# An S5 layer whose inputs and scan states are re-laid by DMAs through DRAM instead of transposes

## The chip, the cores and the metric

The kernel runs on one core of a Trainium2 chip. TensorE multiplies matrices, VectorE and ScalarE work on tiles elementwise, GpSimd does little arithmetic here and issues some of the DMAs, SyncE (SP) issues most of them. Each engine takes its own instructions in their written order and waits on semaphores. The metric is the device time of one execution in microseconds; before the change its median of three runs is 1847.47 us (1845.74 to 1847.80).

## The reference

Two layers over 256 frames of width 2048: gated linear attention, then an S5 state-space layer. The change touches the S5 layer alone:

```python
proj = u_in @ w_in                     # 2048 -> 8192
u, z = jnp.split(proj, 2, axis=-1)     # 4096 each
...
# per group of 16 channels (256 groups, 64 complex states each)
bu = einsum('blgi,gpi->blgp', u_b, B_bar)      # real and imaginary part
x  = associative_scan(x_t = lambda * x_(t-1) + bu_t)
y  = einsum(x_r, c_re) - einsum(x_i, c_im) + d_skip * u
y  = gelu(y)
y  = y * sigmoid(y @ w_glu + b_glu)
y  = y * silu(z)
return y @ w_out                        # then gate, residual, LayerNorm
```

All is float32. A large product is computed from a high part (a rounded copy) and a low part of each operand as three matmuls: high x high, high x low, low x high.

## The kernel before

**Streams of weights.** Each projection runs over groups of 512 output columns. A *step* (a k-pair) loads 512 KB of weights on SP's queue (wload), makes the high part by a ScalarE cast (L145) and the low part by a VectorE subtraction (L146), and then runs 24 TensorE matmuls of 128x256 into four PSUM banks (st_step, L180 to L182). Three buffers each hold high and low parts, so a cast can run three steps ahead of TensorE. S5 has a u stream (tiles wsu, hisu, su; eight groups of eight steps) and then a z stream (wsz, hisz, sz; the same), then the GLU (gl) and the output projection (op).

**The S5 core beside the streams.** The 256 frames are cut into 32 chunks of 8. Index f (0 to 31) stands for 8 channel groups, 128 rows in all. During the u stream:
- s_in copies each u bank out of PSUM with a VectorE transpose (L1108, tile vv), and s_in2, one or two steps later, re-lays it by four TensorE transposes (L1116, psu) and a ScalarE copy (L1118) into Ut, where the 8 frames of a chunk and 16 channels lie on the 128 partitions and the chunks on the free side.
- b_pow and b_tr make the powers of the state matrix times B; s_mm (L1129, L1134) multiplies them with U and writes the chunks' inputs into the state array sx; k_out sends the 8-frame convolution kernel to DRAM (dk) from GpSimd.
- a list of steps is worked off beside the weight steps: bstep takes b_pace of them, pump takes others (scan) at SCAN_RATE.

During the z stream from its second group on, pump works off a list at Y_RATE entries a step. For each f it holds three scan steps (while there are any), cside (loads the convolution matrix mt and the rows cl, and makes the output powers wc on VectorE), xstage and ystage. xstage(f) takes the states of f out of sx by a VectorE transpose (L1245, xT), two TensorE transposes (L1248, psxs) and a ScalarE copy (L1250, xS). ystage(f), two list rounds later, does 48 small matmuls (psy: mt with U at L1260, wc with xS at L1263), a VectorE transpose (yt) and a ScalarE gelu back into Ut. A *y group* is these 48 matmuls, a *state pair* the two transposes. Each z group of four banks ends in four ScalarE silu copies (zs, L1290).

A scheduler, not the source alone, sets the order on each engine: it places an instruction when its inputs are ready by its own estimate. The orders shown below are those of the built programs.

## Time and profile before

| what | value |
| --- | --- |
| median of runs | 1847.47 us |
| span of the profiled execution | 1844.7 us |
| TensorE busy | 1795.5 us (97%) |
| VectorE busy | 1422.5 us (77%) |
| ScalarE busy | 897.4 us (49%) |
| GpSimd busy | 72.7 us (4%) |
| u stream (767.6 to 1036 us) | 268 us |
| z stream (1036 to 1296 us) | 260 us |
| GLU (1296 to 1657 us) | 361 us |

The profiled execution is one run of the program; all durations come from it, and its span, from the first to the last instruction, is 2.8 us under the median of the timed runs. A TensorE instruction's busy time overlaps the next one's: a 128x256 matmul lasts 0.28 us while the following one starts 0.12 us after it. So TensorE time is counted here from start to start.

### The profile page before, as it was taken

To read this page: it belongs to the slowest core of one execution; us is meant where nothing else is said; L and a number is where in the kernel's file an instruction comes from. 1 tells how busy PE (TensorE), PEld (TensorE's weight loads), DVE (VectorE), ACT (ScalarE), POOL (GpSimd) and SP (SyncE) were. 2 spreads that over 40 slices of the span, in tenths; PEclk is the share of its full clock that TensorE was granted. 3 is DMA by queue.
4 is the path that set the end of the run, shared out by engine and by line. 5 is a ranking of instruction groups with operands and counts; after the bars stand their busy time and mean duration, and the time that the engine had idled before them with its cause. 6 is when DMAs were issued, how large, how long until landed. Compare 5 with 4: busy or idle time off the path is not lost.

```text
span 1844.7 us, 33886 instructions
## 1 busy us (share of the span) xinstructions
PE 1795.5 (97%) x13619; PEld 1588.5 (86%) x13619; DVE 1422.5 (77%) x1890; ACT 897.4 (49%) x1252; POOL 72.7 (4%) x78
## 2 busy tenths in 40 slices
PE   7999999999999999999999999999999999999997
PEld 5776897899999888899999999988888888888885
DVE  4877657879989888697899689888677775557556
ACT  5433557556556333654454454545544444444332
POOL 0000000000000000002223200000000000000000
PEclk9999999999999999999999999999999999999999
DMA  9996875889889998465654477899688886668653
GB/s 343 386 333 248 294 244 164 279 261 325 291 286 317 333 353 281 163 220 158 183 151 147 139 214 222 235 246 238 224 276 264 276 271 206 191 189 325 194 184 92
DMA packets 243798, 449.48 MB, mean 244 GB/s; under 512 B 19572, under 2 KB 48942, under 8 KB 242358
## 3 DMA queue, kind: packets, MB, share of 16 engines
q1 hardware_dynamic: 239320, 436.02, 73.9%
q0 software_dynamic: 3552, 10.24, 1.8%
q8 instruction: 107, 1.75, 0.4%
q10 hardware_dynamic: 768, 1.05, 0.2%
q14 instruction: 51, 0.42, 0.1%
HBM read 432.81 MB, written 14.42 MB: 242 GB/s over the span
## 4 chain that ended last, share of the span: by engine, by line
PE 86%; DVE 8%; DMA 3%; ACT 2%; issue 2%; SPq 0%; DVEq 0%; ACTq 0%
PE gl L192 13%; PE gl L193 7%; PE op L168 6%; PE op L167 6%; PE op L169 6%; PE z L182 3%; PE z L180 3%; PE z L181 3%; PE sz L180 3%; PE v L168 3%; PE v L169 3%; PE sz L181 3%; PE sz L182 3%; PE v L167 3%; PE su L180 2%; PE su L182 2%
## 5 line engine op out<-in xcount | busy, mean ns | idle before, releaser
L146 DVE TENSOR_TENSOR logl<-wgl,higl 128x1024 fp32r<-128x1024 f32 x128 | 156.5, 1224 | 115.3 <-ACT higl L145 113.7
L145 ACT CAST higl<-wgl 128x1024 fp32r<-128x1024 f32 x128 | 134.4, 1051 | 172.2 <-PE gl L192 167.9
L192 PE MATMUL gl<-yb,higl 128*128 128x512 f32 x512 | 179.6, 395 | 0.0
L192 PE MATMUL gl<-yp,higl 128*128 128x512 f32 x512 | 179.3, 395 | 0.1
L145 ACT CAST hio<-wo 128x1024 fp32r<-128x1024 f32 x95 | 100.2, 1055 | 155.3 <-PE op L169 127.3
L146 DVE TENSOR_TENSOR loo<-wo,hio 128x1024 fp32r<-128x1024 f32 x95 | 116.2, 1225 | 67.2 <-ACT hio L145 63.7
L315 DVE SCALAR_TENSOR_TENSOR acc<-wa,cs,acc 128x512 f32<-128x512 f32 x217 | 162.2, 748 | 4.8 <-DMA wa<-in_ada_w 2.1
L180 PE MATMUL su<-u1h,hisu 128*128 128x256 f32 x512 | 153.5, 301 | 1.9 <-DVE vv L1108 1.9
L180 PE MATMUL sz<-u1h,hisz 128*128 128x256 f32 x512 | 149.7, 292 | 1.2 <-ACT zs L1290 1.2
L180 PE MATMUL z<-u0h,hiz 128*128 128x256 f32 x512 | 148.7, 290 | 0.0
L182 PE MATMUL su<-u1h,losu 128*128 128x256 f32 x512 | 145.7, 286 | 0.4 <-DVE losu L146 0.4
L181 PE MATMUL su<-u1l,hisu 128*128 128x256 f32 x512 | 145.8, 285 | 0.0
L182 PE MATMUL z<-u0h,loz 128*128 128x256 f32 x512 | 144.9, 283 | 0.6 <-DVE loz L146 0.6
L182 PE MATMUL sz<-u1h,losz 128*128 128x256 f32 x512 | 144.9, 283 | 0.0
L181 PE MATMUL sz<-u1l,hisz 128*128 128x256 f32 x512 | 144.7, 283 | 0.0
L181 PE MATMUL z<-u0l,hiz 128*128 128x256 f32 x512 | 144.7, 283 | 0.0
L193 PE MATMUL gl<-yb,logl 128*128 128x256 f32 x512 | 143.4, 280 | 0.0
L193 PE MATMUL gl<-yp,logl 128*128 128x256 f32 x512 | 142.0, 280 | 0.0
L145 ACT CAST hisz<-wsz 128x1024 fp32r<-128x1024 f32 x64 | 66.9, 1051 | 107.2 <-PE sz L181 55.1
L192 PEld LDWEIGHTS gl<-yb,higl 128*128 128x128 f32 x512 | 96.0, 188 | 22.6
L192 PEld LDWEIGHTS gl<-yp,higl 128*128 128x128 f32 x512 | 95.8, 188 | 22.6 <-issue 0.6
L145 ACT CAST hisu<-wsu 128x1024 fp32r<-128x1024 f32 x64 | 66.7, 1050 | 95.1 <-PE su L181 70.6
(322 smaller groups left out, 5019.8 us busy)
## 6 DMA issues: line engine op xcount, KB each, us to landing
wgl<-in_s_w_glu SPq DMA_DIRECT2D x128, 512.0 KB, 4.7
wa<-in_ada_w SPq DMA_DIRECT2D x116, 512.0 KB, 5.1
wv<-in_gla_w_in SPq DMA_DIRECT2D x64, 512.0 KB, 6.1
wz<-in_gla_w_in SPq DMA_DIRECT2D x64, 512.0 KB, 5.2
wsu<-in_s_w_in SPq DMA_DIRECT2D x64, 512.0 KB, 3.7
wsz<-in_s_w_in SPq DMA_DIRECT2D x64, 512.0 KB, 4.3
wo<-in_s_w_out SPq DMA_DIRECT2D x64, 512.0 KB, 4.5
a<-in_ada_w SPq DMA_DIRECT2D x31, 1024.0 KB, 10.7
```

The lines of the kernel that those rows point to most:

```text
L145: S.copy(hi, w)
L146: last_lo[0] = V.tensor_tensor(lo, w, hi.bitcast(F32), op=ALU.subtract).ins
L167: PE.matmul(banks[tt], lhsT=uh, rhs=hi[:, kk, :], start=(k == first), stop=False)
L168: PE.matmul(banks[tt], lhsT=uh, rhs=lo[:, kk, :], start=False, stop=False)
L169: last_mm[0] = PE.matmul(banks[tt], lhsT=ul, rhs=hi[:, kk, :], start=False, stop=(k == last)).ins
L180: PE.matmul(o, lhsT=wh, rhs=u.hi(k), start=(k == first), stop=False)
L181: PE.matmul(o, lhsT=wh, rhs=u.lo(k), start=False, stop=False)
L182: last_mm[0] = PE.matmul(o, lhsT=wl, rhs=u.hi(k), start=False, stop=(k == last)).ins
L192: PE.matmul(banks[f], lhsT=hi[:, kk, fs], rhs=u.both(k), start=(k == 0), stop=False)
L193: PE.matmul(banks[f][:, :T], lhsT=lo[:, kk, fs], rhs=u.hi(k), start=False, stop=(k == last))
L315: V.scalar_tensor_tensor(acc[0], w[:, kk, :], cs[:, k:k + 1], acc[0], op0=ALU.mult, op1=ALU.add)
```

## The change

**u.** s_in now takes a whole group of four banks. Four ScalarE copies put them, frames within the chunk outermost, into vv (one buffer in place of two); GpSimd issues a DMA of vv to a DRAM scratch du (512 KB) and, when that has landed, a DMA from du into Ut in the wanted layout (runs of 512 bytes). s_in2, its transposes and its copy are gone. Ut's free side is laid out otherwise, so s_mm, ystage and the GLU's conversions address it anew. b_pace starts at -4.0 in place of -1.0, so that s_mm of a group comes three steps later.

**States.** xstage becomes xwrite and xread. xwrite(f) copies the states of f out of sx on ScalarE, with a stride, into xT (one buffer) and GpSimd writes them to the scratch dx (128 KB); xread(f) reads them back into xS (three buffers, runs of 256 bytes). xwrite stands one round ahead of xread, and xread two ahead of ystage. Y_RATE rises from 2.311 to 2.9, as the list grows from 126 entries to 158. yt has one buffer in place of two.

**Rows.** The new layout has another order of the output rows, so rec gets a copy of c's rows with its halves swapped (two more GpSimd writes for each of two halves of the groups), and cload takes one DMA in place of three.

```diff
-    rec = dp.tile([P, 32, 384], F32, name="rec")
+    rec = dp.tile([P, 32, 512], F32, name="rec")
 
     dk = dp.tile([512, 1920], F32, name="dk")
     dxn = dp.tile([T, D], F32, name="dxn")
+    dx = dp.tile([32, P, 256], F32, name="dx")
+    du = dp.tile([8, P, 1024], F32, name="du")
...
-        wdma(rec[:, 16 * t:16 * t + 16, 128:256], lc.rearrange("p f r g n -> p f (r g n)"))
+        wdma(rec[:, 16 * t:16 * t + 16, 256:384], lc.rearrange("p f r g n -> p f (r g n)"))
...
+                if o == 128:
+                    for h in range(2):
+                        wdma(rec[64 * h:64 * h + 64, 16 * t:16 * t + 16, 0:128], av[64 - 64 * h:128 - 64 * h])
...
-    Y_RATE = 2.311
+    Y_RATE = 2.9
...
-    Ut = [s8t(f"U{i}", [8, 2, 128]) for i in range(4)]
+    Ut = [s8t(f"U{i}", [2, 8, 4, 32]) for i in range(4)]
+
+    def Uv(f):
+        return Ut[f // 8][:, (f % 8) // 4, :, f % 4, :]
...
-    def s_in(p, banks):
-
-        v = tp.tile([P, 2, 2, 16, 8], F32, tag="vv", name=f"vv{p}", bufs=2)
-        for i in range(2):
-            V.transpose(v[:, i].rearrange("p b i s -> p s b i"),
-                        banks[i][:, :T].rearrange("p (s b i) -> p s b i", s=8, b=2)[:, ::-1])
-        return v
-
-    def s_in2(p, v):
-        pu = psx(f"psu{p}")
-        for i in range(2):
-            for b in range(2):
-                PE.transpose(pu[:, (2 * i + b) * P:(2 * i + b + 1) * P], v[:, i, b].rearrange("p i s -> p (i s)"), ident)
-        U = Ut[p // 4][:, 2 * (p % 4):2 * (p % 4) + 2]
-        S.copy(U.rearrange("p f b r -> p (f b r)"), pu)
+    def s_in(g, banks):
+
+        v = tp.tile([P, 8, 4, 32], F32, tag="vv", name=f"vv{g}", bufs=1)
+        for i in range(4):
+            S.copy(v[:, :, i], banks[i][:, :T].rearrange("p (s c) -> p s c", s=8)[:, ::-1])
+        wdma(du[g], v.rearrange("p s f c -> p (s f c)"))
+        wdma(Ut[g // 2][:, g % 2].rearrange("p g f c -> p g (f c)"),
+             du[g].rearrange("(g i) (s x) -> (i s) g x", i=16, s=8))
...
-            U = Ut[f // 8][:, f % 8]
+            U = Uv(f)
...
-                    PE.matmul(pss[i][32 * q:32 * q + 32, b * P:(b + 1) * P], lhsT=U[:, b, 32 * q:32 * q + 32],
+                    PE.matmul(pss[i][32 * q:32 * q + 32, b * P:(b + 1) * P], lhsT=U[:, 2 * q + b],
...
-                b_pace[0] = -1.0
+                b_pace[0] = -4.0
...
-        vs.extend((2 * g + i, s_in(2 * g + i, banks[2 * i:2 * i + 2])) for i in range(2))
+        s_in(g, banks)
...
-        dma(a[:, 0:256], rec[:, f, 0:256])
-        for h in range(2):
-            dma(a[64 * h:64 * h + 64, 256:384], rec[64 - 64 * h:128 - 64 * h, f, 0:128])
+        dma(a, rec[:, f, 0:384].rearrange("(r l) x -> l r x", r=4))
...
-    def xstage(f):
-        xt_ = tp.tile([P, 2, 4, 32], F32, tag="xt", name=f"xT{f}", bufs=1)
+    def xwrite(f):
+        xt_ = tp.tile([P, 4, 2, 32], F32, tag="xt", name=f"xT{f}", bufs=1)
         n = 2 * (f % 16)
-        V.transpose(xt_, sx[:, f // 16, 0:32, :, n:n + 2].rearrange("p c r b -> p b r c"))
-        px = psx(f"psxs{f}")
-        for b in range(2):
-            PE.transpose(px[:, b * P:(b + 1) * P], xt_[:, b].rearrange("p r l -> p (r l)"), ident)
-        xs = tp.tile([P, 2, 128], F32, tag="xs", name=f"xS{f}", bufs=2)
-        S.copy(xs, px[:, :T].rearrange("p (b r) -> p b r", b=2))
-        xss[f] = xs
+        S.copy(xt_, sx[:, f // 16, 0:32, :, n:n + 2].rearrange("p c r b -> p r b c"))
+        wdma(dx[f], xt_.rearrange("p r b c -> p (r b c)"))
+
+    def xread(f):
+        xs = xss[f] = tp.tile([P, 4, 2, 32], F32, tag="xs", name=f"xS{f}", bufs=3)
+        wdma(xs.rearrange("p q b c -> p q (b c)"), dx[f].rearrange("(q l) (r x) -> (l r) q x", q=4, r=4))
...
-                    PE.matmul(o[32 * q:32 * q + 32], lhsT=xs[:, b, 32 * q:32 * q + 32],
+                    PE.matmul(o[32 * q:32 * q + 32], lhsT=xs[:, q, b],
...
-        yt = tp.tile([P, 8, 32], F32, tag="yt", name=f"yt{f}", bufs=2)
+        yt = tp.tile([P, 8, 32], F32, tag="yt", name=f"yt{f}", bufs=1)
...
-                if 1 <= f < 33:
-                    bg.append(lambda f=f: xstage(f - 1))
+                for i in range(0 if f == 0 else f + 1, min(f + 2, 32)):
+                    bg.append(lambda i=i: xwrite(i))
+                if f < 32:
+                    bg.append(lambda f=f: xread(f))
...
-                hilo(pr[:, :, 0, :], pr[:, :, 1, :], ysrc[kp // 4][:, sl, :])
+                ph = pr.rearrange("p f h (t c) -> p f h t c", c=32)
+                yu = Ut[kp // 4][:, kp // 2 % 2, :, 2 * (kp % 2):2 * (kp % 2) + 2].rearrange("p t f c -> p f t c")
+                hilo(ph[:, :, 0], ph[:, :, 1], yu)
...
-                    V.tensor_tensor(zs[kp - 12], zs[kp - 12], ysrc[kp - 12], op=ALU.mult)
+                    for h in range(2):
+                        zv = zs[kp - 12][:, 4 * h:4 * h + 4].rearrange("p f (t c) -> p f t c", c=32)
+                        V.tensor_tensor(zv, zv, Ut[kp - 12][:, h].rearrange("p t f c -> p f t c"), op=ALU.mult)
```

The built program has 64 psu and 64 psxs transposes fewer on TensorE, 64 transposes fewer on VectorE and 64 DMAs fewer on SP, and 84 DMAs more on GpSimd.

First place: ScalarE at the end of the third u group (su2). Before, where kT and ks belong to k_out and s_mm and U is written elsewhere from psu:

```order
L145 CAST hisu27_8648<-wsu27_8646 128x1024
L1142 COPY kT2_8319<-pss4_8285 128x256
L1142 COPY kT2_8319<-pss5_8286 128x256
L1153 COPY ks1_8467<-psk1_8462 128x128 x2
L145 CAST hisu30_8701<-wsu30_8699 128x1024
L145 CAST hisu31_8776<-wsu31_8774 128x1024
L1102 COPY wbt4_8584<-pswb80_8585 128x512
```

Now, with the four copies of the finished banks into vv:

```order
L145 CAST hisu32_8733<-wsu32_8731 128x1024
L1143 COPY kT2_8399<-pss4_8365 128x256
L1143 COPY kT2_8399<-pss5_8366 128x256
L1154 COPY ks1_8541<-psk1_8536 128x128 x2
L1116 COPY vv2_8618<-su20_8186 128x8x32
L1116 COPY vv2_8618<-su21_8187 128x8x32
L1116 COPY vv2_8618<-su22_8188 128x8x32
L145 CAST hisu33_8776<-wsu33_8774 128x1024
L1116 COPY vv2_8618<-su23_8189 128x8x32
L1093 COPY wb4_8663<-rb4_8434 128x128 x2
L145 CAST hisu34_8845<-wsu34_8843 128x1024
```

The copies stand after casts of the next group (hisu30 to hisu32), and one cast, hisu33, stands ahead of the last copy. GpSimd's du write and the read into U1 wait for them.

Second place: ScalarE in the z stream, around the last steps of group 4. Before:

```order
L145 CAST hisz44_12974<-wsz44_12972 128x1024
L1267 ACT_TABLE_LOAD
L1267 ACTIVATE U0_7508<-yt7_12772 128x256
L1250 COPY xS9_12820<-psxs9_12817 128x256
L145 CAST hisz45_13042<-wsz45_13040 128x1024
L1267 ACTIVATE U1_7509<-yt8_12847 128x256
L1250 COPY xS10_12895<-psxs10_12892 128x256
L145 CAST hisz46_13117<-wsz46_13115 128x1024
L1267 ACTIVATE U1_7509<-yt9_12922 128x256
L1250 COPY xS11_12970<-psxs11_12967 128x256
L145 CAST hisz47_13182<-wsz47_13180 128x1024
L145 CAST hisz50_13238<-wsz50_13236 128x1024
```

Now, with copies out of sx (xT) that run ahead of the y groups (U<-yt8 and U<-yt9 belong to y groups 8 and 9):

```order
L145 CAST hisz43_12816<-wsz43_12814 128x1024
L1241 COPY xT17_13164<-sx_7511 128x256
L145 CAST hisz44_12884<-wsz44_12882 128x1024
L1262 ACTIVATE U1_7515<-yt8_12699 128x8x32
L1241 COPY xT18_13235<-sx_7511 128x256
L145 CAST hisz45_12947<-wsz45_12945 128x1024
L1241 COPY xT19_13336<-sx_7511 128x256
L1241 COPY xT20_13407<-sx_7511 128x256
L145 CAST hisz46_12988<-wsz46_12986 128x1024
L1262 ACTIVATE U1_7515<-yt9_12800 128x8x32
L1241 COPY xT21_13478<-sx_7511 128x256
L145 CAST hisz47_13056<-wsz47_13054 128x1024
```

The copies from psxs, one for each y group, are gone; the copies xT are closer together than the y groups are, since five of them, xT17 to xT21, stand between hisz43 and hisz47 beside the gelus of two y groups. Each of them waits for the DMA that empties xT. All of xT0 to xT15 stand between the 12th and the 28th cast of the z stream and all of xT16 to xT31 between the 35th and the 48th.

Third place: GpSimd's queue in the same stretch, where nothing stood before:

```order
L1242 DMA dx_200<-xT22_13579 128x256
L1246 DMA xS14_13016<-dx_200 128x4x64
L1242 DMA dx_200<-xT23_13658 128x256
L1242 DMA dx_200<-xT24_13759 128x256
L1246 DMA xS15_13087<-dx_200 128x4x64
L1242 DMA dx_200<-xT25_13830 128x256
L1246 DMA xS16_13167<-dx_200 128x4x64
L1242 DMA dx_200<-xT26_13901 128x256
L1242 DMA dx_200<-xT27_14002 128x256
L1242 DMA dx_200<-xT28_14073 128x256
L1246 DMA xS17_13268<-dx_200 128x4x64
L1242 DMA dx_200<-xT29_14153 128x256
```

Writes of dx and reads of xS alternate. A read waits for its write's landing and for the y group that frees its buffer, three y groups back, and the writes behind it wait with it.

More of the change, by code (lines that the diff above doesn't have):

```diff
@@ L1049, in bload @@
         a = tp.tile([P, 2, 384], F32, tag="rb", name=f"rb{f2}", bufs=2)
-        dma(a[:, :, 0:256], rec[:, 2 * f2:2 * f2 + 2, 128:384])
+        dma(a[:, :, 0:256], rec[:, 2 * f2:2 * f2 + 2, 256:512])
         for h in range(2):
-            dma(a[64 * h:64 * h + 64, :, 256:384], rec[64 - 64 * h:128 - 64 * h, 2 * f2:2 * f2 + 2, 256:384])
+            dma(a[64 * h:64 * h + 64, :, 256:384], rec[64 - 64 * h:128 - 64 * h, 2 * f2:2 * f2 + 2, 384:512])
         rb[f2] = a
@@ L1059, in kload @@
         a = rc[f2] = tp.tile([P, 2, 144], F32, tag="rc", name=f"rc{f2}", bufs=2)
-        dma(a, rec[:, 2 * f2:2 * f2 + 2, 0:144])
+        dma(a, rec[:, 2 * f2:2 * f2 + 2, 128:272])
     wb = {}
@@ L1190, in scan @@
         V.tensor_tensor(N, N, t1[:, 0], op=ALU.add)
-    vs = []
     for g in range(8):
@@ L1199, in trunk @@
             st_step(banks, u1, w, kp, 15)
-            if kp in (0, 2) and vs:
-                s_in2(*vs.pop(0))
             if (g, kp) == (0, 3):
@@ L1280, in trunk @@
             st_step(banks, u1, w, kp, 15)
-            if kp in (0, 2) and vs:
-                s_in2(*vs.pop(0))
             if g == 0:
@@ L1325, in trunk @@
                + [yb[:, i * 2048:(i + 1) * 2048].rearrange("p (k h t) -> p k h t", k=4, h=2) for i in range(4)])
-    ysrc = [u.rearrange("p f b r -> p f (b r)") for u in Ut]
     y2 = Parts([], [])
```

11 lines of the change are left out of this document (5 added, 6 removed).

## The prediction

> **What bounds the kernel now.** I read four views in this order: the chain of waits, the table of stretches, the waits inside the S5 projections, and single timeline stretches of TensorE and GpSimd. The chain comes first because it says whose work sets the end; then one row for each of three stretches of the S5 layer (u projection; first z group; the seven z groups beside which the y matmuls run). Their columns: stretch, its length, busy time of PE, PEld, DVE, ACT and POOL, granted clock, DMA share, GB/s.
>
> ```profile
> PE 86%; DVE 8%; DMA 3%; ACT 2%; issue 2%; SPq 0%; DVEq 0%; ACTq 0%
> ...
> 767.60:1036.00 268.40, 264.04 (x2805) 252.13 (x2803) 239.43 (x327) 137.87 (x250) 51.93 (x49) 0.99 0.56 171
> 1036.00:1069.00 33.00, 32.96 (x368) 31.48 (x366) 15.45 (x17) 17.07 (x33) 11.40 (x15) 1.00 0.44 131
> 1069.00:1296.00 227.00, 220.53 (x2937) 208.20 (x2937) 204.73 (x286) 117.06 (x176) 0.00 (x0) 1.00 0.88 231
> ```
>
> TensorE is idle for 4.4 us of 268 in the u stage and 6.5 of 227 in the y stage. A TensorE instruction taken out there shortens the program by its own pitch, as long as nothing else becomes late. VectorE is second (239 of 268, 205 of 227), ScalarE is half idle, GpSimd idle in the y stage.
>
> **What leaves TensorE.** Three timeline stretches: a u transpose group (L1116), a state transpose pair (L1248) alone, and a pair ahead of a y group.
>
> ```profile
> 842.33 0.28 PE L182 MATMUL su<-u1h,losu 128*128 128x256 f32 x1
> 842.45 0.60 PE L1116 MATMUL psu<-ident,vv 128*128 128x128 f32 x4
> 842.81 0.36 PE L180 MATMUL su<-u1h,hisu 128*128 128x256 f32 x1
> 843.01 0.28 PE L181 MATMUL su<-u1l,hisu 128*128 128x256 f32 x1
> ...
> 1186.56 0.28 PE L182 MATMUL sz<-u1h,losz 128*128 128x256 f32 x1
> 1186.68 0.38 PE L1248 MATMUL psxs<-ident,xT 128*128 128x128 f32 x2
> 1186.82 0.36 PE L180 MATMUL sz<-u1h,hisz 128*128 128x256 f32 x1
> 1187.02 0.28 PE L181 MATMUL sz<-u1l,hisz 128*128 128x256 f32 x1
> ...
> 1177.09 0.28 PE L182 MATMUL sz<-u1h,losz 128*128 128x256 f32 x1
> 1177.21 0.38 PE L1248 MATMUL psxs<-ident,xT 128*128 128x128 f32 x2
> ...
> 1178.97 0.38 PE L180 MATMUL sz<-u1h,hisz 128*128 128x256 f32 x1
> 1179.19 0.28 PE L181 MATMUL sz<-u1l,hisz 128*128 128x256 f32 x1
> ```
>
> Projection matmuls start 0.12 us apart (842.33 to 842.45). The u group delays them by 843.01 - 842.33 - 2 x 0.12 = 0.44 us, and there are 16: 7.0 us. A state pair costs 1187.02 - 1186.56 - 0.24 = 0.22 us, and there are 32: 7.0 us. **14.0 us** of TensorE time goes.
>
> For later: one step (a k-pair, 24 projection matmuls) takes 24 x 0.12 = 2.88 us, and a y group costs 1179.19 - 1177.09 - 0.24 = 1.86 us with its pair, so 1.64 without.
>
> With the transposes go some waits. These rows are from the waits of the S5 projections.
>
> ```profile
> PE pswb L1101 <- DVE wb L1092: 1.9, 2, 1.4
> PE su L180 <- DVE vv L1108: 1.9, 1, 1.9
> PEld psy L1260 <- ACT xS L1250: 1.9, 1, 1.9
> PE psxs L1248 <- DVE xT L1245: 1.2, 2, 0.8
> ```
>
> The last three name removed instructions: 1.9 + 1.9 + 1.2 = **5.0 us**. The first is VectorE's backlog; VectorE loses two groups (below), so some of its 1.9 may go too, but I count none.  Gross gain: **19.0 us**.
>
> **What moves to other engines.** Rows by line for the removed VectorE and ScalarE work, and what the z stream keeps on ScalarE:
>
> ```profile
> L1245 DVE STREAM_TRANSPOSE xT<-sx 128x256 f32<-128x256 f32 x32 | 20.1, 627 | 1.2 <-PE psxs L1248 0.9
> L1108 DVE STREAM_TRANSPOSE vv<-su 128x256 f32<-128x256 f32 x32 | 19.4, 665 | 0.7 <-PE su L182 0.7
> L1250 ACT COPY xS<-psxs 128x256 f32<-128x256 f32 x32 | 11.5, 361 | 2.0 <-PE psxs L1248 2.0
> L1118 ACT COPY U<-psu 128x512 f32<-128x512 f32 x16 | 9.3, 579 | 0.0
> L145 ACT CAST hisz<-wsz 128x1024 fp32r<-128x1024 f32 x53 | 55.4, 1051 | 92.1 <-PE sz L181 48.8 <-issue 36.2 <-DMA wsz<-in_s_w_in 3.5
> L146 DVE TENSOR_TENSOR losz<-wsz,hisz 128x1024 fp32r<-128x1024 f32 x53 | 64.0, 1210 | 7.9 <-ACT hisz L145 6.9 <-PE psy L1260 0.6
> L1267 ACT ACTIVATE U<-yt 128x256 f32<-128x256 f32 x32 | 13.3, 416 | 6.5 <-DVE yt L1266 6.4
> L1267 ACT ACT_TABLE_LOAD x10 | 12.8, 1283 | 5.3 <-DVE yt L1266 5.2
> L1290 ACT ACTIVATE zs<-sz 128x256 f32<-128x256 f32 x25 | 9.1, 387 | 3.9 <-PE sz L182 3.4
> ```
>
> VectorE loses 39.5 us that were beside TensorE; this is cover, not gain. ScalarE's sums hardly change: 32 PSUM copies of 128x256 at the 0.36 of L1250 (11.6 us) for the 9.3 of L1118, and 32 copies out of sx for the 11.5 of L1250. I cost four edits at nothing. The zs product in halves (four instruction starts more) and the y conversions in rows of 32 lie beside the GLU's and the last z group's matmuls; were they bare, four starts of a few tenths each. The four added writes of rec lie beside the v projection, and nothing reads rec before the S5 layer; bare, each is a 512 KB write of some 5 us (below), 20 in all. SP issues 64 loads fewer, beside weights it had loaded in time. What counts is no longer busy time but **two round trips through DRAM**.
>
> GpSimd issues both ways. Its present DMA rows (the last two: a 64 KB write from issue to landing, minimum, median and maximum; a 1 MB one):
>
> ```profile
> 1063.01 0.73 POOL L1159 TENSOR_TENSOR ks<-ks,dm 16x256 f32<-16x256 f32 x1 [1.23 <-ACT ks L1153]
> 1064.03 1.22 POOL L1162 DMA_DIRECT2D dk<-ks  x2 [0.30 <-POOL ks L1159]
> ...
> DMA to landing us min/median/max: 2.1/3.3/5.0
> ...
> rec<-rowsb POOLq DMA_DIRECT2D x2, 1024.0 KB, 7.0
> ```
>
> **u's round trip** is 512 KB out and 512 KB back, in eight groups. Between 3.3 us at 64 KB and 7.0 at 1 MB, 512 KB is about 5.0. In ScalarE's new order one cast (1.05) and the last u copy (0.36) follow the projection's end, so U lands near 1.4 + 5.0 + 5.0 + three handovers of 0.1 to 0.3 = 11.9 us after it. In the new TensorE order 96 projection matmuls, one s_mm (a little over 2 us), 16 weight transposes and four kernel transposes (five groups like the 0.44 above) stand between: 11.5 + 2.1 + 2.2 = 15.8 us; for the last group 72 matmuls, 12.9 us. It is covered, by 3.9 and 1.0 us. I cost it at nothing; its bounds are 0 and, if both ways are as far above 5.0 as the slowest 64 KB write is above the median (5.0 x 5.0 / 3.3 = 7.6), 1.4 + 15.2 + 0.6 = 17.2, so 1.4 us late for seven groups and 4.3 for the last, 14 us. Behind the waiting read in GpSimd's queue stands only the kernel-row work (ks, dk), which nothing waits for before the z stream.
>
> **The states' write** is the place I doubt. xT has one buffer, so each new copy on ScalarE waits until the write of the one before has landed, and behind that waiting copy stand the casts that feed every projection matmul. The period of a copy is T = copy + landing + two handovers.
> - Copy: it reads sx with a stride, 256 elements. Lower bound 0.36 (L1250); upper bound the nearest ScalarE row with a strided SBUF side, which I take, since the VectorE copy of the same pattern is as slow (0.627, L1245): 0.65.
>
> ```profile
> L922 ACT ACTIVATE z<-z x32: 643/666/738, 396.9 to 582.2; 128x256 f32<-128x256 f32 x32
> ```
>
> - Landing of 128 KB in 1 KB rows: bounds 2.1 and 5.0 above; I take the median 3.3, for dk's pair of 64 KB is as large.
> - Handovers: from nothing to 0.3 (POOL row above); 0.1 each.
>
> T = 0.65 + 3.3 + 0.2 = **4.15 us**, between 0.36 + 2.1 = 2.5 and 0.67 + 5.0 + 0.6 = 6.3.
>
> How often does it count? In the new order xT0 to xT15 stand between ScalarE's 12th and 28th cast of the z stream, xT16 to xT31 between the 35th and 48th; that is more than one a step. The three high buffers let a cast run three steps ahead of TensorE. First chain: from the 12th cast (TensorE has done 9 steps) 1.05 + 15 T, 1.5 for a silu group (four L1290 rows) in the middle, 2.1 for the 28th cast and its low half (1.05 + 1.21, less 0.12, since the first two matmuls need the high part alone). TensorE needs 18 steps and 6 y groups: 51.8 + 9.8 = 61.7 us. Late by 15 T - 57.0. Second chain: the write of xT16 waits in GpSimd's queue behind the read of xS10, which needs y group 7, so it starts 1.64 + 0.61 (half the 1.22 of two issues) + 0.4 (handovers of 0.1 and 0.3) = 2.65 us after TensorE's 32nd step, and xT17 is copied at 2.65 + 3.3 + 0.1 = 6.05. Then 14 periods, of which one holds a silu group with two table loads and a cast (5.6 us, not T - 0.65), and 2.75 for the last copy, cast and low half. TensorE needs 15 steps and 12 y groups: 43.2 + 19.7 = 62.9. Late by 13 T - 47.9. Together 28 T - 104.9: at T = 4.15 **11.3 us**; nothing below T = 3.7.
>
> Reading back (xS) has three buffers, so a read is issued three y groups, some 17 us (four steps and three y groups), ahead of its use; even the 5.0 us of the slowest write above is covered.
>
> Sum: -19.0 + 11.3 = -7.7 us. The profiled execution spans 1844.7 us; the median run, 1847.47, is 2.8 above it, and I keep that distance: **1840 us**.
>
> [...]
>
> **The rivals.** That the transposes stay is none: the new program has 128 TensorE and 64 VectorE transposes fewer.
> - *The writes stay hidden.* If T is 3.7 or less, as with the 2.1 us landing (T = 2.95) or the 0.36 copy (T = 3.86, nearly), the whole 19.0 comes: 1828.5; with VectorE's 1.9 as well, 1826.6. For it: GpSimd's queue is empty in the y stage. Against it: a DMA share of 0.88 there, and 0.56 where the 3.3 was taken.
> - *ScalarE becomes the bound of the y stage (slower).* Above T = 4.42 the chains cost more than 19.0. At T = 4.8 (landing 3.95) they cost 29.5: 1858. For it: the y stage carries 256 KB more per y group on queues that are the fullest of the layer. Against it: the median above already stems from loaded queues.
> - *U comes late at s_mm.* At the upper bound the eight groups cost 14 more: -19.0 + 11.3 + 14 = +6.3, 1854. It begins at 12.9 us for the last group and 15.8 for the others, and decides from 17 on. Against it: the margin of 3.9 us.
>
> **How the numbers follow.** Forecast (T from 3.8 to 4.4) 0.42; hidden 0.22; ScalarE bound 0.28; U late 0.08. About 0.2% (3.7 us) is what a measurement tells from no change. The forecast's own range is 1829.5 to 1847 and most of it is faster (0.29, same 0.10, slower 0.03). Faster: 0.29 + 0.22 = 0.51. Same: 0.10 + 0.06 (T near 4.4) + 0.02 = 0.18. Slower: 0.03 + 0.22 + 0.06 = 0.31. The range for 8 in 10 is 1827 to 1861, from hidden writes to T = 4.9.
>
> **What would show it.** Right: no TensorE time at L1116 and L1248; xT copies of about 0.65 us; waits of ScalarE's xT copy for the dx write, and after them TensorE waiting for casts or for the silu that frees its bank, mainly around the 16th to 28th and the 40th to 48th step of z; the u stage some 9 us shorter. Wrong: dx landings under 2.8 us, or over 4; s_mm waiting for U; y groups waiting for xS.

## The result, and the profile after

The changed kernel takes 1897.97 us (median of 4 runs, 1894.85 to 1903.61) against 1846.61: a ratio of 1.0280, interval 1.0259 to 1.0301. The forecast was 1840 us, with a range of 1827 to 1861. Its profiled execution spans 1895.8 us, 51.1 more than that of the kernel before. Measured from the first TensorE instruction of each stream to that of the next, the difference lies so (us):

| stretch | before | after | difference |
| --- | --- | --- | --- |
| up to the u stream | 767.6 | 774.1 | + 6.5 |
| u stream | 268.4 | 260.1 | - 8.3 |
| z stream | 260.1 | 314.3 | + 54.2 |
| GLU | 360.7 | 359.4 | - 1.2 |
| the rest | 188.0 | 187.8 | - 0.2 |

So u's side did what was forecast in its own stage; the loss is in the z stream, and a smaller part lies ahead of the S5 layer. These are the stretches of the kernel after, with the columns of the prediction's table:

```profile
774.10:1034.20 260.10, 255.07 (x2728) 245.05 (x2726) 214.29 (x289) 138.36 (x262) 60.61 (x60) 0.98 0.67 203
1034.20:1067.40 33.20, 32.45 (x361) 30.48 (x358) 18.80 (x21) 15.76 (x30) 12.49 (x16) 1.00 0.52 160
1067.40:1348.40 281.00, 232.16 (x2893) 217.72 (x2893) 193.71 (x264) 121.57 (x179) 44.73 (x70) 0.91 0.78 218
```

The y stage is 281 us long in place of 227; TensorE is idle in 49 of them, where it was in 6.5, and the clock that it was granted is 0.91 in place of 1.00. The waits of the z stream say what each engine waited for (us in total, times, longest):

```profile
POOL dx L1242 <- ACT xT L1241: 103.4, 26, 6.3
ACT xT L1241 <- DMA dx<-xT: 89.4, 28, 6.6
POOL xS L1246 <- PE psy L1258: 83.0, 15, 9.5
DVE losz L146 <- ACT hisz L145: 71.9, 30, 7.8
...
PE sz L180 <- ACT zs L1283: 25.5, 5, 9.8
...
PE psy L1255 <- DMA mt<-dk: 11.4, 6, 3.4
```

ScalarE's copies of the states wait for the write of the one before 28 times. Behind them the silus that free TensorE's banks come late, five times, up to 9.8 us. The next lines show the copies, and the time of their writes from issue to landing (minimum, median, maximum):

```profile
L1241 ACT COPY xT<-sx x32: 621/653/692, 1075.0 to 1257.7; 128x256 f32<-128x256 f32 x32
...
DMA to landing us min/median/max: 2.0/3.9/7.1
```

The copies come in the two chains that the order showed: xT0 at 1075.0 to xT15 at 1150.79, and xT16 at 1180.24 to xT31 at 1257.7. That is 75.8 / 15 = 5.05 and 77.5 / 15 = 5.16 us a copy: the prediction's T, taken there as 4.15.

One stall shows how this works. These are the timelines of TensorE and of ScalarE, and the stretches around the stall:

```profile
1101.63 0.28 PE L182 MATMUL sz<-u1h,losz 128*128 128x256 f32 x1
1107.56 0.58 PE L180 MATMUL sz<-u1h,hisz 128*128 128x256 f32 x1 [5.65 <-ACT zs L1283]
1107.94 0.41 PE L181 MATMUL sz<-u1l,hisz 128*128 128x256 f32 x1
1108.15 0.41 PE L182 MATMUL sz<-u1h,losz 128*128 128x256 f32 x1
```
```profile
1101.90 0.62 ACT L1241 COPY xT<-sx 128x256 f32<-128x256 f32 x1 [3.37 <-DMA dx<-xT]
1102.43 1.04 ACT L145 CAST hisz<-wsz 128x1024 fp32r<-128x1024 f32 x1
1106.59 0.63 ACT L1241 COPY xT<-sx 128x256 f32<-128x256 f32 x1 [3.12 <-DMA dx<-xT]
1107.12 0.93 ACT L1283 ACTIVATE zs<-sz 128x256 f32<-128x256 f32 x3
```
```profile
1101.00:1105.70 4.70, 0.91 (x8) 0.71 (x6) 2.73 (x5) 1.57 (x2) 1.30 (x2) 1.00 0.91 269
1105.70:1112.50 6.80, 4.94 (x34) 4.67 (x38) 5.43 (x12) 5.29 (x9) 0.54 (x1) 0.50 0.57 164
```

The silu stands behind the copy xT6, the copy behind the landing of xT5. And the stall costs twice: from 1105.7 to 1112.5 the granted clock is 0.50, and the matmuls that follow start 0.21 us apart in place of 0.12. Over the z stream, gaps between TensorE's starts that are over 0.3 us longer than usual add up to 51.7 us (6.9 before), and matmuls at half clock lose another 14.7 (0 before). So the stalls grew by 44.8 us. With the 14.7, less the 7.0 us of the state pairs that are gone, plus 1.1 of u-side work that moved into this stream, that makes 53.6 of the 54.2 us.

### The profile page after: what moved, and what is told of

It is laid out like the page before. It is cut to its first block, busy times and chain, and to the rows that moved or that the text cites. A ratio compares the mean times of both kernels' runs of the same rounds, so it can differ in the third digit from the quotient of the medians.

```text
span 1895.8 us, 33645 instructions
## 1 busy us (share of the span) xinstructions
PE 1799.6 (95%) x13491; PEld 1591.7 (84%) x13491; DVE 1386.3 (73%) x1830; ACT 899.9 (47%) x1262; POOL 130.4 (7%) x162
## 5 line engine op out<-in xcount | busy, mean ns | idle before, releaser
L180 PE MATMUL sz<-u1h,hisz 128*128 128x256 f32 x512 | 154.9, 303 | 30.5 <-ACT zs L1283 25.5
L182 PE MATMUL sz<-u1h,losz 128*128 128x256 f32 x512 | 149.5, 293 | 6.8 <-DVE losz L146 6.8
L181 PE MATMUL sz<-u1l,hisz 128*128 128x256 f32 x512 | 149.1, 291 | 0.0
L180 PEld LDWEIGHTS sz<-u1h,hisz 128*128 128x128 f32 x512 | 102.6, 200 | 39.1 <-ACT zs L1283 26.6
L146 DVE TENSOR_TENSOR losz<-wsz,hisz 128x1024 fp32r<-128x1024 f32 x64 | 77.4, 1216 | 71.9 <-ACT hisz L145 71.9
L192 PEld LDWEIGHTS gl<-yp,higl 128*128 128x128 f32 x512 | 95.9, 188 | 22.8 <-issue 0.7
```

Source lines behind the costliest of these rows:

```text
L146: last_lo[0] = V.tensor_tensor(lo, w, hi.bitcast(F32), op=ALU.subtract).ins
L180: PE.matmul(o, lhsT=wh, rhs=u.hi(k), start=(k == first), stop=False)
L181: PE.matmul(o, lhsT=wh, rhs=u.lo(k), start=False, stop=False)
L182: last_mm[0] = PE.matmul(o, lhsT=wl, rhs=u.hi(k), start=False, stop=(k == last)).ins
L192: PE.matmul(banks[f], lhsT=hi[:, kk, fs], rhs=u.both(k), start=(k == 0), stop=False)
```

## The experiments

The theory to begin with: the single xT buffer and ScalarE's order make the loss. The rivals are that the two sides hurt each other, that U comes late, and that the transfers themselves are too slow.

**Each part alone.** These are three kernels: u's side alone (the states' code, rec, cload and the list's rate of the kernel before), the states' side alone, and the kernel before with nothing but the added writes (their lines are shown).

```diff
 # rec alone: kernel before
+                if o == 128:
+                    for h in range(2):
+                        wdma(rec[64 * h:64 * h + 64, 16 * t:16 * t + 16, 0:128], av[64 - 64 * h:128 - 64 * h])
```

> Only u's side of the change (dense ScalarE copies, du out and back, U in the new layout, b_pace from -4.0); the states go by VectorE and TensorE transposes as before, with rec, cload and the rate of the y list as before. Theory (the loss is all on the states' side: ScalarE's xT copies wait for the write before to land, 5.1 us a copy in the changed kernel's two runs of copies): the u stage comes down from 268.4 us to about 260, the y stage stays at its 260 us, so 1846.6 - 9 = 1838 us. Rival (u's round trip is what costs, its s_mm late and the stream behind it pushed): 1850 or more, with TensorE waiting for U.

> Only the states' side of the change (xT copied by ScalarE, dx out and back, the rows of rec four times, the list at 2.9); u goes by transposes as before. Theory: the whole loss is here, + 54 us in the z stream and + 6 ahead of the S5 layer: 1846.6 + 60 = 1907 us, with waits of the xT copy for the dx write of some 90 us. Rival (the two sides hurt each other, by GpSimd's queue and the DMA engines that they share): well under 1890.

> The kernel before with the four added writes of c's rows to rec, which nothing reads; all else as before. The changed kernel is 6.3 us behind at the start of the first layer's z stream, with TensorE stalls of 2.4 and 2.8 us and two half-clock stretches of 3.4 us that were not there before. Theory (the added writes delay the weights of the v and z streams): + 6 us, 1852.5. Rival (the order or chance put them there, the writes are hidden as the prediction had it): 1846.6 within 1.5.

Measured: u's side 1845.55 against 1846.10, ratio 0.9988 (0.9974 to 1.0002); the states' side 1903.24, 1.0304 (1.0282 to 1.0325); the added writes 1852.44, 1.0035 (1.0021 to 1.0050). The loss is that of the states' side (which has the added writes too), with no part of it from the two together. The writes that the prediction held for covered cost 6.3 us. No engine waits for them; the weights beside them come late. Two lines of that kernel's timelines (ScalarE, TensorE) and two stretches at half clock show it:

```profile
368.88 1.99 ACT L145 CAST hiz<-wz 128x1024 fp32r<-128x1024 f32 x2 [8.06 <-DMA wz<-in_gla_w_in]
...
371.73 1.33 PE L849 MATMUL psst<-qs,qk 128*64 128x256 f32 x8 [2.53 <-ACT sts L853]
```
```profile
314.40:317.80 3.40, 3.40 (x13) 2.88 (x13) 3.31 (x7) 1.75 (x3) 0.00 (x0) 0.50 0.49 154
...
372.40:375.80 3.40, 3.40 (x19) 2.66 (x16) 3.33 (x5) 2.28 (x9) 0.00 (x0) 0.50 1.04 376
```

The cast waits 8.06 us for its weights (4.1 before), behind it the copies sts come late, and TensorE stalls. Seven of the nine profiled kernels with these writes in the v projection have both half-clock stretches there; none of the others has one. In the changed kernel they begin at 313.8 and 371.8 us and last 3.4 us each.

u's side met neither its theory (1838) nor its rival (1850 or more): it gains 8.0 us in the u stream (260.4), and loses most of it again, since the z stream is 266.9 in its profile.

**ScalarE out of the chain.**

```diff
-        S.copy(xt_, sx[:, f // 16, 0:32, :, n:n + 2].rearrange("p c r b -> p r b c"))
+        nc.gpsimd.tensor_copy(xt_, sx[:, f // 16, 0:32, :, n:n + 2].rearrange("p c r b -> p r b c"))
```

> The changed kernel, with the copy of the states out of sx made by GpSimd in place of ScalarE; buffers, writes, reads and everything else stay. It takes the wait for the dx write out of ScalarE's order, so casts and silus no longer stand behind it; the transfers are the same. Theory (ScalarE's order is the path): the y stage's stalls of TensorE (51.7 us in the changed kernel, 6.9 before) and the 14.7 us that its matmuls lose at half clock go, 1898 - 50 = about 1845 to 1850. Rival (the transfers themselves, mt's loads or the reads of xS are late, whoever copies): it stays above 1880, with TensorE waiting for mt or xS. If GpSimd's own turn (copy, write, landing, read) becomes longer than a y group's period of 7 us, y groups wait for xS: 1870 or so.

Measured: 1898.82, 1.0290 (1.0267 to 1.0312). ScalarE no longer waits, and nothing is gained; the stalls are 51.7 us again. Two waits in its z stream are:

```profile
POOL xT L1241 <- DMA dx<-xT: 108.0, 30, 7.5
...
PE psy L1258 <- DMA xS<-dx: 31.5, 7, 8.1
```

GpSimd now stands where ScalarE stood, and the reads of xS behind it come late, so the y groups wait. This is the third outcome of the expectation, and dearer than the 1870 given there. ScalarE's order was only the way in which the one-buffer round trip reached TensorE.

**When the copies are asked for.** In the changed kernel the scheduler drew the copies forward to one behind each cast. The first kernel ties each copy to the cast of its own step, which keeps the copies in the list's order (spread). The second has two buffers each for xT and xS besides, and the third has the buffers alone.

```diff
+        last_hi[0] = S.copy(hi, w).ins          # in split
...
+        with tc.issue_after(last_hi[0]):
             S.copy(xt_, sx[:, f // 16, 0:32, :, n:n + 2].rearrange("p c r b -> p r b c"))
...
-    xt_ = tp.tile(..., tag="xt", bufs=1)         # second and third kernel
+    xt_ = tp.tile(..., tag="xt", bufs=2)
-    xs = xss[f] = tp.tile(..., tag="xs", bufs=3)
+    xs = xss[f] = tp.tile(..., tag="xs", bufs=2)
```

> The changed kernel, with one thing more: each copy of the states (xT) keeps its place in the written list behind the cast of the same step, where the scheduler had drawn the copies forward (one behind every cast of the z stream's second and third group, and one behind nearly every cast again from the fifth). Now they come one in about two casts, some 6.5 us of TensorE time apart. Buffers and transfers are as in the changed kernel. Theory (a copy needs 5.1 us because of the one xT buffer, and the order asks for one every 2.9 to 4 us: bunching): most of the 45 us of added stalls and of the 14.7 us at half clock go, 1898 - 50 = 1848, and with the transposes' 14 us already out, 1843 to 1852. Rival (the round trips through DRAM themselves or the load on the DMA engines are too slow): 1880 or more.

> As the kernel with spread copies, with two xT buffers and two xS buffers in place of one and three. Theory (bunching at one buffer): nothing is left for the second xT buffer to gain, and two xS buffers still give a read some two y groups (13 us) against its 5.8 us: within 4 us of the spread kernel. Rival (ScalarE's wait costs even when the copies are spread): faster than it by 5 us or more. If a read has too little lead with two buffers, y groups wait for xS and it is slower.

> The changed kernel with two xT buffers and two xS buffers in place of one and three, the copies not held back. In its order the scheduler now puts two copies behind each cast where it put one. Theory (bunching): two copies per cast with two buffers need the same 5.1 us a cast as one with one, for half as many casts: half of the loss stays, with y groups waiting for xS because its reads stand in GpSimd's queue behind more writes: 1870 to 1900. Rival (the single buffer alone is at fault): 1850 or less.

Measured: spread 1876.36, 1.0151 (1.0134 to 1.0169); spread with two and two buffers 1861.53, 1.0074 (1.0058 to 1.0090); the buffers alone 1882.34, 1.0185 (1.0168 to 1.0203). The tie is worth 21.6 us, not the 45 to 50 expected, and the second buffer another 14.8, where nothing was expected: its rival holds. In the spread kernel (the tie alone) ScalarE still waits 77.2 us for the write, which lands later there (median 4.8, 3.9 in the changed kernel). The buffers alone, with two copies behind each cast in the order, give 15.6. In the spread kernel with two and two buffers another wait has taken over:

```profile
PE psy L1256 <- DMA mt<-dk: 16.2, 10, 3.5
...
ACT xT L1242 <- DMA dx<-xT: 3.9, 4, 2.6
```

**Who issues the writes.** Here the writes are issued from ScalarE's queue, in the changed kernel and in the spread one with two and two buffers:

```diff
-        wdma(dx[f], xt_.rearrange("p r b c -> p (r b c)"))
+        nc.scalar.dma_start(dx[f], xt_.rearrange("p r b c -> p (r b c)"))
```

> The changed kernel with the dx writes issued by ScalarE, right behind each copy, in place of GpSimd; reads stay on GpSimd. Theory (bunching, a copy's period is copy 0.65 + handover 0.3 + landing 3.9 + 0.1): the handover goes and the landing stays, so 0.3 x 28 = 8 us less: about 1889. Rival 1 (GpSimd's queue holds the writes up, behind reads that wait for y groups 83 us in all): 1860 or less, and the copies' second run begins earlier. Rival 2 (ScalarE's own queue lands much faster, near the 2.2 us of its 64 KB output rows): period 3.2 us, loss gone, 1850.

> The kernel with spread copies, two xT and two xS buffers, with the dx writes issued by ScalarE in place of GpSimd. Where ScalarE issued them before, a write landed in 2.6 us in the median (3.9 from GpSimd in the changed kernel, 6.2 in the kernel with spread copies and two and two buffers). Theory (what is left there, 22 us of stalls and 9 us at half clock, comes from mt's loads and from VectorE at the head of the z stream, no longer from the states' write): within 4 us of its 1861.5. Rival (late writes still hold up the reads and with them the y groups): 1850 or less.

Measured: 1892.94, 1.0239 (1.0220 to 1.0259), and 1863.65, 1.0092 (1.0064 to 1.0121). The waits and the landing of the first of the two kernels:

```profile
ACT xT L1241 <- DMA dx<-xT: 75.6, 22, 7.0
...
DMA to landing us min/median/max: 1.7/2.6/5.1
```

The 2.6 us here, which two later expectations take for an earlier landing, comes from only five of the 32 writes: for the others the trace ties no landing to the issue. The DMA packets of all 32 show that the last packet of a write ended 3.4 us after the issue in the median. In the changed kernel a landing comes some 0.4 us behind the last packet, so its 3.9 are about 3.5 by this measure: the write lands no earlier. The copies still wait 22 times, 3.4 us on average, and T is 4.5 in the first chain and 5.0 in the second. What went is the handover from copy to issue (0.29 us from GpSimd, 0.03 here): 5 us gained, near the theory's 8. Where the copies hardly wait any more, in the second kernel, the other queue gains nothing. That sets GpSimd's queue aside as the cause.

**The added writes elsewhere.** Here two 1 MB copies in the u stage take the place of the four writes, on the spread kernel with two and two buffers:

```diff
-                        wdma(rec[64 * h:64 * h + 64, 16 * t:16 * t + 16, 0:128], av[64 - 64 * h:128 - 64 * h])
+                    wdma(rec[64 * h:64 * h + 64, :, 0:128], rec[64 - 64 * h:128 - 64 * h, :, 128:256])   # after s_in(0)
```

> The kernel with spread copies, two xT and two xS buffers, with the four added writes of rec taken out of the v projection and made as two 1 MB copies from DRAM to DRAM in the u stage, behind the first read of U on GpSimd's queue. Theory (the added writes cost 6.4 us because the v stage has no DMA time left, a share of 0.85; the u stage has 0.56 to 0.67): 1861.5 - 6 = 1855.5. Rival (they only move: the weights of the u stage or its second U come late): 1861 or more.

Measured: 1854.41, 1.0039 (1.0016 to 1.0062). That is 7.1 us less than without this edit, and the first layer's z stream begins at 369.6. The theory holds.

**The load on the DMA engines.** What remains are y groups that wait for mt. The next rows are of the kernel before, of the spread kernel with two and two buffers, and of the one with rec's copies moved as well. They show mt's time to landing, the stretch from 1070 to 1290 us (its last two numbers are DMA share and GB/s), and in the third the waits for mt.

```profile
DMA to landing us min/median/max: 6.7/7.1/7.3
1070.00:1290.00 220.00, 213.53 (x2844) 201.53 (x2843) 197.79 (x274) 111.42 (x168) 0.00 (x0) 1.00 0.89 234
```
```profile
DMA to landing us min/median/max: 7.2/9.4/10.2
1070.00:1290.00 220.00, 204.03 (x2628) 193.52 (x2630) 176.38 (x241) 111.16 (x162) 42.19 (x65) 0.97 0.96 260
```
```profile
DMA to landing us min/median/max: 7.8/9.6/10.7
...
PE psy L1259 <- DMA mt<-dk: 19.4, 10, 3.8
```

The trace ties a landing to only three to five of the 32 mt loads of a kernel, so these medians are rough. By the packets of all 32 (mt's are the only 4 KB packets on SP's queue in this stage), the last one ends 6.2 us after the issue in the median before, and 8.2 and 8.1 in the other two. An mt buffer is free again when y group f - 2 is through, and y group f mostly comes 8 to 13 us later (in the kernel before 23 times of 30, median 11.3); the shorter landings fit into that, the longer ones often don't. Three more kernels bear on it. Two have the traffic of dx and xS on the kernel before (with one yt buffer, as in the change), and one has half of mt's bytes on the kernel with rec's copies moved; its matmuls take the four frames twice, so it leaves out half of the convolution:

```diff
 # load_only: behind S.copy(xs, ...)
+        wdma(dx[f], xs.rearrange("p b r -> p (b r)"))
+        wdma(dump, dx[f].rearrange("(q l) (r x) -> (l r) q x", q=4, r=4))
 # load2: behind the gelu
+        wdma(dx[f], U.rearrange("p b r -> p (b r)"))
+        if f >= 4:
+            wdma(dump, dx[f - 4].rearrange("(q l) (r x) -> (l r) q x", q=4, r=4))
 # mthalf
-        src = ... ap=[[1920, 16], [128, 8], [1, 1024]]
+        src = ... ap=[[1920, 16], [128, 8], [1, 512]]
```

> The kernel before, and beside each xS copy a write of it to DRAM (128 KB) and a read of that into a tile that nobody uses: the traffic of dx and xS, issued by GpSimd, without any engine that waits for it. TensorE, VectorE, ScalarE and SP keep their order. Theory (part of the loss is load: with 256 KB more per y group the 512 KB loads of mt land in 9.4 us instead of 7.1, and their two buffers leave 9 to 11): mt lands 1.5 to 2.3 us later, TensorE waits for it some 8 to 15 us more than the 3.9 before, 1846.5 + 10 = 1855. Rival (only the waits on the round trips cost, the traffic itself fits into a share of 0.88): 1846.5 within 2.

> The kernel with spread copies, two and two buffers and rec's rows copied in the u stage, with mt's load cut to its first four of eight frames (256 KB); the matmuls take these four twice, so their number and shape stay, and y is not the reference's. Theory (mt's late loads, 19.4 us of TensorE's waits there, and the half-clock stretches behind them, 8.6 us, are what is left): 1854.4 - 20 = 1834. Rival (another late input takes their place, xS or cl): 1850 or more.

> The kernel before with traffic alone, made so that no engine but GpSimd waits for it (in the first try ScalarE's xS copies waited 37.8 us for the write): behind each gelu a 128 KB write of its U, which nothing overwrites, and a 128 KB read of what was written four groups earlier into a tile that nobody uses; 28 reads. TensorE, VectorE, ScalarE and SP keep their order. Theory (load on the DMA engines: a share of 0.89 before and of 0.96 in the best variants of the states' side, mt landing in 7.1 and 9.4 us): the share rises to about 0.95, mt lands 1.5 to 2.5 us later, TensorE waits for mt 8 to 15 us more, and the time is 1846.4 + 8 to + 20. Rival (only waits on the round trips cost; the first try's loss was ScalarE's wait): 1846.4 within 3.

The first gave 1870.64, 1.0140 (1.0119 to 1.0160), but it doesn't show what it was to show: its single dump tile held GpSimd's queue up, and ScalarE's next xS copy waited for the write, 37.8 us in all, so it is the round trip once more. In the second no engine but GpSimd waits for the traffic in the y stage; of its 1873.61, 1.0151 (1.0135 to 1.0168), 15 us lie in the GLU, whose start waits for the last of GpSimd's queue. What counts is its z stream: 265.5 us, against 260.1 and 259.2 in two executions of the kernel before. Its rows for mt are:

```profile
PE psy L1261 <- DMA mt<-dk: 1.8, 3, 1.2
...
DMA to landing us min/median/max: 8.2/8.7/8.8
```

So under the load alone (a DMA share of 0.95) mt lands later, by 1.6 us in these three landings and by 0.8 in the packets of all 32 (median 7.0). The stream is some 5 to 6 us longer in this one profile, less than the 8 to 20 of the theory, and TensorE's waits for mt don't grow: the loads still just fit. Half of mt's bytes gave 1831.58, 0.9922 (0.9905 to 0.9939):

```profile
PE psy L1259 <- DMA mt<-dk: 1.2, 1, 1.2
...
DMA to landing us min/median/max: 3.6/4.9/5.5
```

This is 22.8 us less than with all the bytes: the waits for mt (19.4 to 1.2) and the half-clock losses (8.6 to 1.3) are gone, at a DMA share of 0.81. That this is near the prediction's case of hidden writes (1828.5) proves nothing: u's side nets far less than was counted there, and what the kernel before would gain from half of mt's bytes was not tried. Since the last packet comes later in the states' variants (8.1 to 8.2) than with the bare traffic (7.0), load alone isn't the whole of it; what adds the rest was not tried.

**u's round trip.** Three kernels have u's side alone, with s_mm one step earlier, with the du writes issued by ScalarE besides, and with these writes alone:

```diff
-                b_pace[0] = -4.0
+                b_pace[0] = -3.0                        # u_pace, u_act
-        wdma(du[g], v.rearrange("p s f c -> p (s f c)"))
+        nc.scalar.dma_start(du[g], v.rearrange("p s f c -> p (s f c)"))   # u_act, u_act4
```

> Only u's side of the change, with b_pace from -3.0 in place of -4.0, so s_mm one step (2.88 us) earlier. In the u-only kernel the u stage is 8.2 us shorter, but the z stream 6.8 us longer: 1.1 by work that moved there and some 5 by a stall of 3.6 us at its second group's head, where VectorE is late, with a half-clock stretch after it. U lands 11.9 us after a projection's end (group 0 of the changed kernel: 802.5 to 814.3), s_mm comes at 15.8 and would come at 12.9. Theory (the delay of b_pace pushes powers of the state matrix into the z stream's head): U still is in time and a part of the 5 us goes: 1841 to 1844. Rival (the margin is used up, s_mm waits for U): 1846 to 1850.

> Only u's side, b_pace from -3.0, with the du writes issued by ScalarE in place of GpSimd. With GpSimd's writes s_mm waited 12.6 us for U at this pace (up to 3.6 for a group) and the median was 1854.85. A write of 128 KB landed 1.3 us sooner from ScalarE than from GpSimd. Theory (U's round trip is the only thing in the way): each of the six late groups gains 1 to 2 us, 1846 to 1849. If ScalarE's queue gains more than 3 us a group: 1842, and faster than the kernel before. Rival (512 KB land no sooner, the bytes rule): 1854.

> Only u's side, du written by ScalarE, b_pace from -4.0 as in the change. With -3.0 it takes 1843.95 and s_mm still waits 5.5 us for U. Theory (that wait is the rest): without it 5 us less in the u stage, but powers of the state matrix three steps later, as in the u-only kernel: 1840 to 1844. Rival (what the step saves in the u stage comes back at the z stream's head, as with -4.0 before): 1844 to 1846.

Measured: 1854.85, 1.0042 (1.0024 to 1.0061); 1843.95, 0.9978 (0.9961 to 0.9996); 1845.19, 0.9994 (0.9983 to 1.0005). With s_mm one step earlier (the first kernel), TensorE waits for U:

```profile
PE pss L1127 <- DMA U<-du: 12.6, 6, 3.6
```

With ScalarE's writes (the second) 5.5 of it remain. This is the only kernel with the reference's result that is faster than the one before, by 0.2%, at the edge of what can be told. With s_mm where the change has it (the third) the u stream is 260.6 and the z stream 261.8 in the profile, 6 us less than before together, but the median shows 1. What single profiles are worth, the next run tells:

> The kernel before once more, for a second profiled execution. In its first the first layer's z stream began at 368.8 us; in the four kernels with only u's side changed, whose first layer is instruction for instruction the same, it began at 372.5 to 373.6. Theory (executions of one program differ by some 5 us there, and the comparison of single profiles is that uncertain): 367 to 375, other than 368.8 by a microsecond or more. Rival (the changed programs are slower there for a reason of their own, as by another place of their tensors in DRAM): 368.8 within 0.5.

Measured: 1847.74, 1.0001 (0.9985 to 1.0017). These are the first layer's z matmuls (first and last start) in the first execution and in this one:

```profile
L180 PE MATMUL z<-u0h,hiz x512: 280/283/681, 368.8 to 581.6; 128*128 128x256 f32 x171
```
```profile
L180 PE MATMUL z<-u0h,hiz x512: 278/283/681, 373.2 to 586.0; 128*128 128x256 f32 x171
```

The stream's start moves by 4.4 us by itself. Single profiles are that uncertain ahead of S5; on the changed kernel's 6.5 us there, only the timed runs with rec's writes can speak.

**All four edits** (tie, buffers, ScalarE's writes, rec's copies) stand together in the last kernel, with b_pace from -3.0:

> All four edits together on the changed kernel: spread copies, two xT and two xS buffers, dx writes from ScalarE, rec's swapped rows copied in the u stage, b_pace from -3.0. If each brings what the theories say: 1861.5 - 6 (rec) - 3 (b_pace) = 1852, still slower than the kernel before, since mt's loads stay late. If late writes were the rest: 1840.

Measured: 1865.82, 1.0108 (1.0079 to 1.0137). TensorE waits for U again (10.0 us in the u stream, 3.4 behind it) and mt is late as ever (19.5). This kernel is 11.4 us slower than the one with rec's copies moved. Elsewhere the earlier s_mm cost 9.3 us (u's side alone) and ScalarE's writes 2.1 (two and two buffers), which would make up the 11.4; here the two were not separated.

## Why the prediction was wrong

- **The period T** is the step that failed first. The copy was right (0.653 us for 0.65). The landing was put at the 3.3 us of writes in the u stage, under a DMA share of 0.56; in the y stage it is 3.9 in the median and up to 7.1. The two handovers took 0.3 and 0.1 in place of 0.1 each, and T is 5.05 and 5.16 in place of 4.15. The prediction's own formula gives 28 x 5.1 - 104.9 = 37.9 us for that, of 44.8 measured as stalls, where 11.3 were forecast. The mechanism, its place and its two chains were right, its size was not; the rival that makes ScalarE the bound named it, but stopped at T = 4.8. The row against the choice was in view: the share of 0.88, quoted there against the hidden case only. A median landing of 3.9 even lies within the limits (2.8 to 4) that the prediction gave for being right.
- **Half clock** was no term at all. It took 14.7 us in the z stream, where the stretches at 0.50 came at the stalls: with them the 44.8 us of added stalls cost some 1.3 times their length.
- **Four edits at nothing:** the writes of rec cost 6.3 us by themselves (20 had been given as their bare price). The cover named, the v projection, was none, as weights had to arrive beside them (a cast waited 8.06 us for its weights, 4.1 before). The GLU's conversions and the zs halves are indeed hidden: the GLU takes 359.4 us against 360.7.
- **u.** The gross gain in the u stage is 8.3 us, where 9 were forecast. s_mm starts 15.2 us after the projection's end in the first group (15.8 forecast). But U lands 10.5 to 16.2 us after the end, in place of 11.9: the read alone is issued 5.6 to 11.4 us after it, and in the slower groups kernel-row work stands ahead of u's transfers in GpSimd's queue; the prediction looked only at what stands behind. So the margin of 3.9 is nearly used up: 0.9 us of waits with the change's delay, 12.6 with one step less (u's side alone). That u's side then nets no more than 2 us is explained only in part, by u-side work in the z stream and by a gap of 3.6 us at its second group's head, where TensorE waits for VectorE and half clock follows.
- **xS covered:** true while the reads are free to go. GpSimd waits 83.0 us for y groups before a read, as foreseen for the second chain, and no y group of the changed kernel waits for xS.
- **What was left out:** the 256 KB more per y group as a load on other transfers. TensorE waits 11.4 us for mt in the changed kernel (3.9 before), and 16.2 to 19.4 when the copies hardly stall any more.

Between the forecast (7.7 us less) and the measured spans (51.1 more) lie 58.8 us. T's size makes 26.6 of them by the prediction's formula, stalls beyond the formula 6.9, half clock 14.7, and the stretch ahead of S5 6.5.

Taken off step by step in the runs, the order of the copies is worth 21.6 us, the second buffer 14.8 and rec 7.1. What is left is 8 above the kernel before in place of 14 to 19 below it; with half of mt's bytes another 22.8 go. The new rate of the list (2.9) was not varied alone.

## What to carry to other kernels

Price a round trip through DRAM by landings in the stage where it will run, at that stage's DMA share (here the median was 3.3 us for 64 KB at a share of 0.56, and 3.9 for 128 KB at 0.75), and look in the new order how often it is asked for: here a scheduler that drew copies forward, to one in 2.9 to 4 us where the list has one in some 6.5, turned a period that is long enough on average into a stall nearly each time (28 waits of 32 copies). A transfer that nobody waits for wasn't free where the stage already waited for DMAs: the four writes of rec cost 6.3 us beside a cast that had waited 4.1 us for its weights before. Count long TensorE stalls at more than their length: here 44.8 us of added ones came with a loss of 14.7 at half clock. Use two executions before reading differences of 5 us out of single profiles (the same program's z stream began 4.4 us apart in two), and see how many transfers a median of landings stands for.

## What the runs showed of the hardware

**Half clock after short stalls.** In the z stream of the changed kernel eight gaps between two TensorE starts are 2.7 us long or longer: 4.06, 5.92, 10.11, 2.70, 8.43, 2.87, 3.38 and 3.81 us. With seven of them a stretch at a granted clock of 0.50 begins, within the gap (four) or 0.3 to 1.6 us behind its end (three); the eighth (3.81) falls into one. The longest of these stretches begins only 0.07 us into its gap of 8.43, so what came just before it, gaps of 1.78 and 1.04, may have brought it. Gaps away from these stretches are 1.51 us long at most. The seven stretches last 3.4 us (twice), 6.8 (three times), 10.2 and 13.7. In the kernel before, the longest gap of the z stream is 2.21 us, and the clock stays at 1.00 there. Outside the z streams no one length parts gaps with a stretch from those without: a gap of 2.14 us in the u stream of the kernel before had a stretch 1.4 us behind it, gaps of 2.27 and 2.32 us in its first layer had none, and one of 2.39 in the changed kernel's first layer had one 0.8 us behind it.

**The landing of one size of write varied.** A 128 KB write of the states took 2.0 to 8.6 us from GpSimd, its median 3.9, 4.8 and 6.2 in the changed, the spread and the spread kernel with two and two buffers, whose DMA shares were 0.75, 0.87 and 0.94 (1067 to 1280 us), but 3.8 at 0.86 with the buffers alone, so the share over this stretch doesn't set it alone (there all the writes were issued by 1211 us). From ScalarE, in the changed kernel with its writes, the last packet ended 1.3 to 6.8 us after the issue, and its median of 3.4 us is about that of GpSimd's writes (3.9 less 0.4); the handover was 0.29 us from GpSimd and 0.03 from ScalarE.
